# Weights, sums of squares and key products leave GpSimd for ScalarE and VectorE

## The chip, the cores and the metric

The kernel runs on one core of a Trainium2 chip. The metric is the device time of one launch in microseconds, as a median of several runs. TensorE is PE in the profile (its weight loads are PEld), VectorE is DVE, ScalarE is ACT, GpSimd is POOL and SyncE, which issues all of this kernel's DMAs, is SP.

## The reference

One inference step of a two-layer decoder trunk, in fp32, for a prompt of 1024 tokens and a group of 8 samples of 8 tokens; the model width is 1024. Every sub-layer is wrapped in two norms, and each layer ends in a feed-forward part (ffn) with a causal convolution of three taps:

```python
def rmsnorm(x, g):
    y = x32 * lax.rsqrt(jnp.mean(x32 * x32, axis=-1, keepdims=True) + EPS)
    return (y * g.astype(jnp.float32)).astype(x.dtype)

def conv_ffn(h, buf, w_up, dw_w, dw_b, w_down):          # D 1024, D_FF 2816
    up = h @ w_up
    c, buf_new = causal_dwconv(up, buf, dw_w, dw_b)
    g, val = jnp.split(c, 2, axis=-1)
    return (jax.nn.gelu(g) * val) @ w_down, buf_new

for layer in range(DEPTH):                               # in trunk
    h = rmsnorm(x, p['norm_pre_mix'][layer])
    y = even_mixer(...) if layer % 2 == 0 else odd_mixer(...)
    x = x + rmsnorm(y, p['norm_post_mix'][layer])
    h = rmsnorm(x, p['norm_pre_ffn'][layer])
    f, fb = conv_ffn(h, ...)
    x = x + rmsnorm(f, p['norm_post_ffn'][layer])
```

Layer 0's mixer is a gated linear attention (4 heads) beside a convolution of 31 taps over 512 channels; layer 1's is a dilated window attention in three groups (window 128, 512, 2048) beside a gated spatial product (gmlp). In layer 1 the samples' queries also meet the keys and values of three caches:

```python
s = jnp.einsum('bqhd,bqjhd->bqhj', qb, kv_sel[:, :, :, 0]) + bias_hj      # in dilated_attn
```

## The kernel before

The activations lie transposed, channels on the 128 partitions and tokens along the free axis. The tokens are worked in two halves: A is 512 tokens of the prompt; B is the other 512 and the 64 sample tokens, 576 columns, which every product takes in two pieces of 288.

**Products in fp32 from rounded parts.** Each product with a weight (`gemm`, L374) splits both operands into a rounded high part and the rest, and sums three products: high x high, low x high, high x low. The activations are split by `split` (L402: `hi` on ScalarE, `lo` on VectorE). The weights are split as they come, by `chunk` (L355) and `fill` (L363): the weight's DMA into `raw` (two buffers), the rounding into `whi` (three buffers), and the subtraction `wlo = raw - whi` (three buffers). A chunk is 128 x 1024 for an input or up projection, 128 x 512 or 128 x 384 for a down projection. Two counters out of 16 say which engine rounds and which subtracts: `hi_act` is the share of roundings on ScalarE (the rest go to GpSimd, `gts`, L206), `lo_pool` the share of subtractions on GpSimd (the rest go to VectorE). They change by stage in `run` (L1854): at the start 0 and 0; from the second part of the first input projection to the end of layer 0's ffn of A, 16 and 8; then 0 and 0; in layer 1's input projection of B, `hi_act` is 6; from the output projection of B in layer 1 to the end of layer 1's ffn of A, 16 and 16; then 0 and 0 to the end.

**Norms.** `sq_add` (L415) adds the squares of eight tiles for a norm: ScalarE squares, then a sum is added to a running tile `ss`. Where a half is not marked `urgent` there is one running tile, and GpSimd adds. Where it is marked, the norm is one that the next products wait for, and there are two running tiles, one added by GpSimd and one by VectorE. `rb` (L437) then multiplies each tile with a column of ones on TensorE, per block of 128 tokens, takes the reciprocal root (`rstd`, L229, on GpSimd) and spreads it. `last_down` (L644) does the sums for the last norm by itself, in two tiles, on GpSimd (L699).

**Keys of the cache.** `sample_scores` (L1676) multiplies cached keys `kc` with rows of queries on GpSimd (L1692) and reduces each product on VectorE (L1696). It runs beside layer 1's input projection of B, and its tiles come by DMA from the caches and from the queries in DRAM, up to `SA` tiles ahead.

**Order.** Work that is not a product of the main line (the convolution, linear attention, attention, norms) is a generator, woven between the products by `during` and `pump` (L236, L242) at a rate per product, and finished by `drain`. Each engine's order of instructions is then planned from estimated times, by priority; `chunk` puts its fills up to `ahead` = 400 places forward. On the chip every engine takes its list in that order.

Work that stays on GpSimd: small copies of the ffn's convolution edges (L600, L605, L606, L617, L618), the powers in `rstd`, scalings of the attention's scores (`gts` at L1466 and L1503), and memsets.

Of the kernel before, what the change touches and what calls it, by code (L numbers as in the profile page):

```python
# [9 lines left out]
F32 = mybir.dt.float32  # L10
# [3 lines left out]
ALU = mybir.AluOpType  # L14
# [124 lines left out]
class Kern:  # L139
    def __init__(self, ctx, tc, I, O):  # L140
        self.tc, self.nc, self.I, self.O = tc, tc.nc, I, O
        self.uid = 0
        pool = lambda name, **kw: ctx.enter_context(tc.tile_pool(name=name, **kw))
        self.cp = pool("cp", bufs=1)
        self.dp = pool("dp", bufs=1, space=DRAM)
        self.ar = [pool("arA", bufs=24), pool("arB", bufs=24)]
        self.wp = pool("wp", bufs=3)
        self.ap = pool("ap", bufs=10)
        self.fp = pool("fp", bufs=2)
        self.np_ = pool("np", bufs=1)  # L150
        self.mp = pool("mp", bufs=2)
        self.pg = pool("pg", bufs=4, space=PSUM)
        self.pm = pool("pm", bufs=4, space=PSUM)
        self.halves = [Half(0), Half(1)]
        self.rr = 0
        self.copy_act = False
        self.urgent = [0, 0]
        self.bg = None
        self.ahead = 0

        self.nw, self.hi_act, self.lo_pool = 0, 0, 0


    def nm(self, s):
# [197 lines left out]

    def fill(self, raw, whi, wlo, w, k0, nk, c0, m):  # L363
        self.wdma(raw[:, :nk, :m], w[k0 * P:(k0 + nk) * P, c0:c0 + m].rearrange("(k p) m -> p k m", p=P))
        self.nw += 1
        if self.nw * self.hi_act % 16 < self.hi_act:
            self.acopy(whi[:, :nk, :m], raw[:, :nk, :m])
        else:
            self.gts(whi[:, :nk, :m], raw[:, :nk, :m], 1.0, 0.0)
        eng = self.nc.gpsimd if self.nw * self.lo_pool % 16 < self.lo_pool else self.nc.vector  # L370
        eng.tensor_tensor(out=wlo[:, :nk, :m], in0=raw[:, :nk, :m], in1=whi[:, :nk, :m].bitcast(F32),  # L371
                          op=ALU.subtract)

    def gemm(self, h, hs, w, k0, c0, m):  # L374

# [38 lines left out]

    def sq_add(self, h, ss, src, k):  # L415

        if len(ss) <= k and len(ss) <= self.urgent[h.i]:
            ss.append(self.at(h, [P, h.n], name="ss") if self.urgent[h.i] else
                      self.np_.tile([P, h.n], F32, tag="ss", name=self.nm("ss"), bufs=2))
            self.act(ss[-1], src, AF.Square)  # L420
            return
        sq = (self.at(h, [P, h.n], name="sq") if self.urgent[h.i] else
              self.np_.tile([P, h.n], F32, tag="sq", name=self.nm("sq"), bufs=1))
        self.act(sq, src, AF.Square)
        t = ss[k % len(ss)]
        eng = self.nc.vector if k % len(ss) else self.nc.gpsimd
        eng.tensor_tensor(out=t, in0=t, in1=sq, op=ALU.add)  # L427

    def rms(self, h, src):

# [213 lines left out]
    def last_down(self, h, tmp, acts, l, part, y, xt):  # L644


        w = self.I["w_down"][l]
        nk = len(part)
        wts = []
        for m in range(KT):  # L650
            raw = self.wp.tile([P, 8, P], F32, tag="raw", name=self.nm("raw"), bufs=2)
            wt = [self.at(tmp if m < KT - 2 or not i else h, [P, nk, P], F32R, name="wt") for i in range(2)]
            self.fill(raw, wt[0], wt[1], w, part[0], nk, m * P, P)
            wts.append(wt)

        def rows(blocks, c1, sq):

            ps = self.psm()
            for b in blocks:
                c0, sz = h.blocks[b]  # L660
                for i, t in enumerate(sq):
                    self.mm(ps[:sz, b:b + 1], t[:, c0 - c1:c0 - c1 + sz], self.ones[:, :1], i == 0, i == len(sq) - 1)
            r = self.np_.tile([P, 8], F32, tag="r", name=self.nm("r"), bufs=2)
            full = [b for b in blocks if b < 4]
            self.rstd(r[:, full[0]:full[-1] + 1], ps[:, full[0]:full[-1] + 1], 1.0 / D)
            if 4 in blocks:
                self.rstd(r[:NS, 4:5], ps[:NS, 4:5], 1.0 / D)
            yield 1.0
            for b in blocks:
                c0, sz = h.blocks[b]  # L670
                for hf in range(2):
                    ps = self.psm()
                    for kk in range(4):
                        self.tr(ps[:sz, kk * P:(kk + 1) * P], y[hf * 4 + kk][:, c0:c0 + sz])
                    ob = self.at(h, [P, 512], name="ob")
                    self.stt(ob[:sz, :], ps[:sz, :], r[:sz, b:b + 1], xt[b][hf][:sz, :], ALU.mult, ALU.add)
                    if b < 4:
                        dst = self.O["y_prompt"][0, h.t0 + c0:h.t0 + c0 + sz, hf * 512:hf * 512 + 512]
                    else:
                        dst = self.O["y_sample"].rearrange("b s d -> (b s) d")[:, hf * 512:hf * 512 + 512]  # L680
                    self.dma(dst, ob[:sz, :])
                yield 1.0

        for blocks in ([2, 3, 4], [0, 1]):
            c1 = h.blocks[blocks[0]][0]
            cw = sum(h.blocks[b][1] for b in blocks)
            sqs = []
            for m in range(KT):
                ps = self.pg.tile([P, 512], F32, tag="g", name=self.nm("g"))
                for k in range(nk):  # L690
                    for j, (i, e) in enumerate(((0, 0), (0, 1), (1, 0))):
                        self.mm(ps[:, :cw], wts[m][i][:, k, :], acts[part[k]][e][:, c1:c1 + cw],
                                k == 0 and j == 0, k == nk - 1 and j == 2)
                yv = y[m][:, c1:c1 + cw]
                self.tt(yv, yv, ps[:, :cw], ALU.add)
                sq = self.at(h, [P, cw], name="sq")
                self.act(sq, yv, AF.Square)
                if m % 4:
                    self.nc.gpsimd.tensor_tensor(out=sqs[-1], in0=sqs[-1], in1=sq, op=ALU.add)  # L699
                else:  # L700
                    sqs.append(sq)
                self.acopy(yv, yv, self.v("norm_post_ffn", l * KT + m))
                self.pump(nk / 8 * cw / 512)
            self.during(rows(blocks, c1, sqs), len(blocks) + 1, 1.5)
        self.drain()
# [970 lines left out]
    def sample_scores(self, h, st):  # L1676


        nc = self.nc
# [3 lines left out]
        for stk in range(2):  # L1683
            sT = self.at(h, [P, 2, P], name="sT")
            st["sT"].append(sT)
            sv = sT.rearrange("p g (b h q) -> p g b h q", b=4, h=4)
            for bl in range(4):
                for z in range(4):
                    kc, qt = take(4 * stk + bl, 0, z)
                    for k, q in enumerate(qt):  # L1690
                        pr = self.wk(1 + (2 * z + k) % 4, [P, 512])
                        nc.gpsimd.tensor_tensor(out=pr, in0=kc.rearrange("p i c -> p (i c)"),  # L1692
                                                in1=q.rearrange("p i c -> p (i c)"), op=ALU.mult)
                        q0 = 2 * (z % 2) + 4 * k
                        dst = sv[:, z // 2, bl, :, q0:q0 + 2].rearrange("p h q -> p q h")
                        nc.vector.reduce_sum(out=dst, in_=pr.rearrange("p (i h d) -> p i h d", i=2, h=4), axis=AX.X)  # L1696
                        yield 1.0

            nc.vector.tensor_copy(sv[:, 1, :, :, 4:], sv[:, 1, :, :, :4])
# [154 lines left out]
    def run(self):  # L1854
# [27 lines left out]
        self.ahead = 400  # L1882
        self.drain()
        self.mix_consts()
        self.hi_act, self.lo_pool = 16, 8
        self.during(self.conv(A, st[0]), 90, 30)
        self.in_even(A, st[0]["hs"], st[0], ("glr", "q", "k", "v0", "v1", "r"))
        rest = self.merge((self.bg, 50), (self.gla(A, st[0]), 45))
# [17 lines left out]
        self.during(mix0(), 210, 61)  # L1906
        y, ss = self.ffn(A, hA, 0)
        self.drain()
        self.hi_act, self.lo_pool = 0, 0
        hA = []  # L1910
        self.urgent[0] = 1
        for _ in norms(A, y, ss, 1, "norm_post_ffn", 0, "norm_pre_mix", 1, hA):
# [41 lines left out]
        def odd_b():  # L1954
            self.drain()
            self.urgent = [0, 0]
            act = lambda shape: self.ap.tile(shape, F32, tag="act", name=self.nm("sg"))
            self.copy_act, self.hi_act = True, 6
            so[1] = self.in_odd(B, hB, lambda st: self.during(self.merge((self.gmlp(B, st, act), 11), (self.sample_scores(B, st), 48)), 59, QS))
            self.drain()  # L1960
            self.ffn_rows(0)
            self.copy_act, self.hi_act = False, 0
            self.during(mix1(B), QM, 45)

        def close_b():
            self.drain()
            self.hi_act, self.lo_pool = 16, 16
            y, ss = self.out_proj(B, so[1]["mo"], I["w_out_odd"][0])
            nxt["hB"] = []
            self.urgent[1] = 1  # L1970
# [2 lines left out]
        y, ss = self.ffn(A, nxt["hA"], 1, {0.5: odd_b, 4: close_b})  # L1973
        self.drain()
        self.urgent = [0, 0]
        self.hi_act, self.lo_pool = 0, 0
        rows = []

        def end_a():
# [34 lines left out]
```

## Time and profile before

| | us |
|---|---|
| median of 3 runs | 2743.83 |
| lowest, highest | 2738.05, 2746.66 |
| the profiled execution | 2735.78 |
| its span, first to last instruction | 2733.9 |
| mean granted clock of TensorE | 0.97 |

A line of the profile names a source line, an engine, an operation and the tiles it writes and reads (`out<-in`), with the count behind an x. "Idle before" and "waits" say how long an engine stood before an instruction and what released it. PEclk, or the clock in a window, is the share of full speed that TensorE was granted. A window is a stretch of the span in us.

### The profile page before, as it was taken

Reading aid. Unit: us, or ns where it says so; the run is one execution under the profiler, and the core shown is the slowest. Engines: PE = TensorE matmul, PEld = TensorE weight load, DVE = VectorE, ACT = ScalarE, POOL = GpSimd, SP = SyncE. Lnnn points to the kernel's source line nnn. Section 1 sums busy time; section 2 is a strip of 40 time slices with the busy share of each in tenths; the row PEclk is TensorE's granted clock in tenths of the full one; section 3 lists DMA queues with packets and bytes.
Section 4 is the critical chain, followed back from the end, with each engine's and each line's share of the span. In section 5 each row is a group of like instructions: output and inputs, shape, how many; then the busy total and the mean of one; then the engine's idle time right before and its main releaser. Section 6 shows DMA issues by size and latency. Waiting matters only on the chain.

```text
span 2733.9 us, 43963 instructions
## 1 busy us (share of the span) xinstructions
PE 2601.8 (95%) x16517; PEld 2327.2 (85%) x16517; DVE 1753.5 (64%) x3065; ACT 961.9 (35%) x2022; POOL 1023.1 (37%) x1139
## 2 busy tenths in 40 slices
PE   7989999999999999999999999889999898999998
PEld 6779787787888779999999979878878678999998
DVE  4897359999677653655557784547665358555555
ACT  4343445443453222333323242113333343322223
POOL 2311333342235443243437533553113266333333
PEclk9999989999999999999999999999999799999999
DMA  7433354454544454332324336884454152422232
GB/s 218 127 99 92 90 188 151 138 159 159 179 142 126 152 179 117 117 97 81 89 70 137 122 112 191 234 237 133 131 162 137 34 172 84 140 78 75 81 91 82
DMA packets 505004, 355.83 MB, mean 130 GB/s; under 512 B 29547, under 2 KB 461282, under 8 KB 504015
## 3 DMA queue, kind: packets, MB, share of 16 engines
q1 hardware_dynamic: 504791, 353.01, 42.7%
q8 instruction: 131, 2.15, 0.3%
q14 instruction: 82, 0.67, 0.1%
HBM read 306.43 MB, written 75.97 MB: 140 GB/s over the span
## 4 chain that ended last, share of the span: by engine, by line
PE 73%; DVE 10%; DMA 7%; POOL 4%; issue 3%; ACT 2%; SPq 1%; DVEq 0%; POOLq 0%; ACTq 0%
PE g L227 65%; PE m L227 7%; DVE cv L200 3%; PE m L224 2%; DMA kc<-qr 2%; DVE wlo L371 1%; SPq L188 1%; POOL whi L206 1%; DVE y L200 1%; DVE c L200 1%; POOL ss L427 1%; POOL w L1692 1%; DVE lo L197 1%; DVE y L197 1%; POOL wlo L371 1%
## 5 line engine op out<-in xcount | busy, mean ns | idle before, releaser
L227 PE MATMUL g<-hi,whi 128*128 128x288 f32 (+2 forms) x4440 | 1276.7, 336 | 25.7 <-DVE y L197 9.3
L227 PE MATMUL g<-lo,whi 128*128 128x288 f32 (+2 forms) x4440 | 1263.5, 333 | 5.4 <-DVE lo L197 5.3
L227 PE MATMUL g<-hi,wlo 128*128 128x288 f32 (+1 forms) x4416 | 1254.4, 333 | 9.8 <-POOL wlo L371 6.6
L227 PEld LDWEIGHTS g<-hi,whi 128*128 128x128 f32 (+1 forms) x4440 | 776.5, 191 | 100.0 <-issue 25.9
L227 PEld LDWEIGHTS g<-lo,whi 128*128 128x128 f32 (+1 forms) x4440 | 775.3, 191 | 69.2 <-DVE lo L197 7.5
L227 PEld LDWEIGHTS g<-hi,wlo 128*128 128x128 f32 x4416 | 771.5, 191 | 72.5 <-POOL wlo L371 7.0
L371 DVE TENSOR_TENSOR wlo<-raw,whi 128x1024 fp32r<-128x1024 f32 (+2 forms) x382 | 408.1, 1069 | 443.0 <-POOL whi L206 346.1
L206 POOL TENSOR_SCALAR whi<-raw 128x1024 fp32r<-128x1024 f32 (+2 forms) x307 | 313.7, 1022 | 708.8 <-PE g L227 589.2
L371 POOL TENSOR_TENSOR wlo<-raw,whi 128x1024 fp32r<-128x1024 f32 (+2 forms) x94 | 205.0, 2182 | 417.0 <-ACT whi L209 357.1
L200 DVE SCALAR_TENSOR_TENSOR c<-u,dw,c 128x512 f32<-128x512 f32 (+3 forms) x528 | 318.7, 641 | 47.1 <-ACT c L212 45.7
L209 ACT ACTIVATE whi<-raw 128x1024 fp32r<-128x1024 f32 (+3 forms) x171 | 145.1, 849 | 362.8 <-PE g L227 189.4
L209 ACT ACTIVATE u<-g 128x224 f32<-128x224 f32 (+2 forms) x352 | 128.7, 397 | 299.9 <-PE g L227 286.4
L200 DVE SCALAR_TENSOR_TENSOR cv<-u,cvw,cv 128x512 f32<-128x512 f32 (+21 forms) x240 | 193.3, 815 | 1.8
L197 DVE TENSOR_TENSOR y<-y,g 128x288 f32<-128x288 f32 (+3 forms) x240 | 120.3, 526 | 107.2 <-PE g L227 106.9
L212 ACT ACTIVATE c<-g,dw 128x288 f32<-128x288 f32 (+1 forms) x264 | 172.9, 657 | 2.6 <-DVE lo L197 1.5
L427 POOL TENSOR_TENSOR ss<-ss,sq 128x512 f32<-128x512 f32 (+1 forms) x75 | 120.8, 1611 | 42.7 <-ACT sq L212 41.4
L209 ACT ACTIVATE hi<-c 128x512 fp32r<-128x512 f32 (+1 forms) x88 | 57.9, 658 | 209.1 <-DVE c L197 208.7
L212 ACT ACTIVATE c<-c 128x512 f32<-128x512 f32 (+1 forms) x88 | 57.9, 658 | 142.2 <-DVE c L200 138.3
L600 POOL COPY last<-u 128x2 f32<-128x2 f32 x88 | 49.9, 568 | 120.8 <-ACT u L209 118.0
L200 DVE SCALAR_TENSOR_TENSOR y<-y,vec,rb 128x512 f32<-128x512 f32 (+1 forms) x104 | 88.3, 915 | 7.1 <-ACT rb L209 7.1
L212 ACT ACTIVATE sq<-y 128x512 f32<-128x512 f32 (+3 forms) x103 | 63.1, 622 | 82.9 <-POOL ss L427 43.9
L1692 POOL TENSOR_TENSOR w<-kc,kc 128x512 f32<-128x512 f32 x48 | 65.2, 1372 | 70.7 <-DMA kc<-qr 58.6
(288 smaller groups left out, 2208.7 us busy)
## 6 DMA issues: line engine op xcount, KB each, us to landing
raw<-in_w_up SPq DMA_DIRECT2D x176, 512.0 KB
raw<-in_w_down SPq DMA_DIRECT2D x128, 256.0 KB
raw<-in_w_in_odd SPq DMA_DIRECT2D x44, 512.0 KB
raw<-in_w_in_even SPq DMA_DIRECT2D x40, 512.0 KB
out_s_kv<-in_cache_c_w SPq DMA_DIRECT2D x32, 512.0 KB
raw<-in_w_down SPq DMA_DIRECT2D x64, 192.0 KB
xl<-x SPq DMA_DIRECT2D x40, 256.0 KB
kc<-in_cache_c_w SPq DMA_DIRECT2D x80, 128.0 KB
```

Source lines behind the costliest of these rows:

```text
L188: self.nc.sync.dma_start(out, in_)
L197: self.nc.vector.tensor_tensor(out=out, in0=a, in1=b, op=op)
L200: self.nc.vector.scalar_tensor_tensor(out=out, in0=a, scalar=s, in1=b, op0=op0, op1=op1)
L206: self.nc.gpsimd.tensor_scalar(out=out, in0=a, scalar1=s1, scalar2=s2, op0=op0, op1=op1)
L209: self.nc.scalar.activation(out, in_, AF.Copy, scale=scale)
L212: self.nc.scalar.activation(out, in_, func, **kw)
L224: self.nc.tensor.transpose(out, in_, self.ident[:k, :k])
L227: self.nc.tensor.matmul(out, l, r, start=start, stop=stop)
L371: eng.tensor_tensor(out=wlo[:, :nk, :m], in0=raw[:, :nk, :m], in1=whi[:, :nk, :m].bitcast(F32), op=ALU.subtract)
L427: eng.tensor_tensor(out=t, in0=t, in1=sq, op=ALU.add)
L600: self.nc.gpsimd.tensor_copy(self.last2[l][:, jt, :], u[:, 512:514])
L1692: nc.gpsimd.tensor_tensor(out=pr, in0=kc.rearrange("p i c -> p (i c)"), in1=q.rearrange("p i c -> p (i c)"), op=ALU.mult)
```

## The change

All roundings of weights go to ScalarE and all their subtractions to VectorE, whatever the stage, and the two counters go. A norm has one running tile in all cases, and VectorE adds to it; so it does in `last_down`. The keys' products go to VectorE.

```diff
     def fill(self, raw, whi, wlo, w, k0, nk, c0, m):
         self.wdma(raw[:, :nk, :m], w[...].rearrange("(k p) m -> p k m", p=P))
-        self.nw += 1
-        if self.nw * self.hi_act % 16 < self.hi_act:
-            self.acopy(whi[:, :nk, :m], raw[:, :nk, :m])
-        else:
-            self.gts(whi[:, :nk, :m], raw[:, :nk, :m], 1.0, 0.0)
-        eng = self.nc.gpsimd if self.nw * self.lo_pool % 16 < self.lo_pool else self.nc.vector
-        eng.tensor_tensor(out=wlo[:, :nk, :m], in0=raw[:, :nk, :m], in1=whi[:, :nk, :m].bitcast(F32),
-                          op=ALU.subtract)
+        self.acopy(whi[:, :nk, :m], raw[:, :nk, :m])
+        self.tt(wlo[:, :nk, :m], raw[:, :nk, :m], whi[:, :nk, :m].bitcast(F32), ALU.subtract)
...
     def sq_add(self, h, ss, src, k):
-        if len(ss) <= k and len(ss) <= self.urgent[h.i]:
+        if not ss:
...
-        t = ss[k % len(ss)]
-        eng = self.nc.vector if k % len(ss) else self.nc.gpsimd
-        eng.tensor_tensor(out=t, in0=t, in1=sq, op=ALU.add)
+        self.tt(ss[0], ss[0], sq, ALU.add)
...
                 if m % 4:                                   # last_down
-                    self.nc.gpsimd.tensor_tensor(out=sqs[-1], in0=sqs[-1], in1=sq, op=ALU.add)
+                    self.tt(sqs[-1], sqs[-1], sq, ALU.add)
...
                         pr = self.wk(1 + (2 * z + k) % 4, [P, 512])      # sample_scores
-                        nc.gpsimd.tensor_tensor(out=pr, in0=kc..., in1=q..., op=ALU.mult)
+                        self.tt(pr, kc..., q..., ALU.mult)
```

The lines of `run` that set `hi_act` and `lo_pool` go as well.

More of the change, by code (lines that the diff above doesn't have):

```diff
@@ L159, in __init__ @@
         self.ahead = 0
-        self.nw, self.hi_act, self.lo_pool = 0, 0, 0
     def nm(self, s):
@@ L1691, in sample_scores @@
                         pr = self.wk(1 + (2 * z + k) % 4, [P, 512])
-                        nc.gpsimd.tensor_tensor(out=pr, in0=kc.rearrange("p i c -> p (i c)"),
-                                                in1=q.rearrange("p i c -> p (i c)"), op=ALU.mult)
+                        self.tt(pr, kc.rearrange("p i c -> p (i c)"), q.rearrange("p i c -> p (i c)"), ALU.mult)
                         q0 = 2 * (z % 2) + 4 * k
@@ L1884, in run @@
         self.mix_consts()
-        self.hi_act, self.lo_pool = 16, 8
         self.during(self.conv(A, st[0]), 90, 30)
@@ L1908, in run @@
         self.drain()
-        self.hi_act, self.lo_pool = 0, 0
         hA = []
@@ L1957, in odd_b @@
             act = lambda shape: self.ap.tile(shape, F32, tag="act", name=self.nm("sg"))
-            self.copy_act, self.hi_act = True, 6
+            self.copy_act = True
             so[1] = self.in_odd(B, hB, lambda st: self.during(self.merge((self.gmlp(B, st, act), 11), (self.sample_scores(B, st), 48)), 59, QS))
@@ L1961, in odd_b @@
             self.ffn_rows(0)
-            self.copy_act, self.hi_act = False, 0
+            self.copy_act = False
             self.during(mix1(B), QM, 45)
@@ L1966, in close_b @@
             self.drain()
-            self.hi_act, self.lo_pool = 16, 16
             y, ss = self.out_proj(B, so[1]["mo"], I["w_out_odd"][0])
@@ L1975, in run @@
         self.urgent = [0, 0]
-        self.hi_act, self.lo_pool = 0, 0
         rows = []
```

## The prediction

> **What bounds the kernel now.** I read the page's engine totals first, then its slices, then the waits of TensorE, then stretches of time.
>
> ```profile
> span 2733.9 us, 43963 instructions
> PE 2601.8 (95%) x16517; PEld 2327.2 (85%) x16517; DVE 1753.5 (64%) x3065; ACT 961.9 (35%) x2022; POOL 1023.1 (37%) x1139
> ...
> PEclk9999989999999999999999999999999799999999
> ```
>
> TensorE is the bound: 95% of the span, the next engine 64%. Only its holes (132 us) and its slow stretches (the slices with a 7, 8 or 9 for the clock) can be won; work of the other engines costs something only where it makes a hole. Both kinds of stretch, and the places that matter below, by windows (width; busy PE, PEld, DVE, ACT, POOL; granted clock; DMA):
>
> ```profile
> 375.00:389.00 14.00, 11.07 (x52) 10.83 (x51) 3.34 (x5) 1.66 (x3) 6.98 (x4) 0.63 0.81 278
> 536.00:550.00 14.00, 7.38 (x21) 5.55 (x20) 12.00 (x22) 4.04 (x8) 10.99 (x5) 0.63 0.35 114
> 883.00:902.00 19.00, 13.65 (x76) 13.18 (x75) 11.28 (x9) 2.08 (x4) 12.96 (x9) 0.73 0.32 102
> 2234.00:2254.00 20.00, 16.48 (x62) 13.25 (x61) 16.02 (x24) 9.79 (x17) 12.66 (x14) 0.74 0.65 223
> 410.00:684.00 274.00, 260.19 (x1293) 209.98 (x1292) 262.77 (x475) 117.62 (x193) 94.86 (x57) 0.96 0.47 152
> 684.00:820.00 136.00, 136.00 (x689) 112.18 (x687) 90.58 (x163) 64.66 (x128) 40.69 (x46) 1.00 0.51 160
> 1709.00:1845.00 136.00, 116.79 (x778) 108.04 (x777) 70.62 (x119) 25.70 (x66) 69.69 (x61) 0.95 0.85 236
> 2330.00:2660.00 330.00, 329.10 (x2478) 328.79 (x2477) 175.45 (x298) 93.08 (x230) 116.29 (x205) 1.00 0.31 91
> ```
>
> The last row has 330 us with no hole at all: nothing can be won there. The first four are the places where TensorE waits for GpSimd. Who it waits for, by its own waits (total us, times, longest):
>
> ```profile
> PE g L227 <- DVE y L197: 10.6, 5, 4.1
> PE m L227 <- POOL ss L427: 9.8, 3, 3.5
> PE g L227 <- ACT hi L209: 6.7, 4, 3.0
> PE g L227 <- POOL wlo L371: 6.6, 1, 6.6
> PE g L227 <- ACT c L212: 6.1, 2, 5.2
> ```
>
> Each of those waits is paid twice: behind it the clock is granted at less than full. In the four windows the share missing is 0.37x14, 0.37x14, 0.27x19 and 0.26x20, that is 5.2 us of full speed in each.
>
> **Why those waits exist.** The costliest forms of what moves, with mean ns (line, engine, shape, count | busy us, mean ns | idle before), then the subtraction's durations (shortest, median, longest, all and in 410 to 684) and single instructions (start, us):
>
> ```profile
> L371 DVE TENSOR_TENSOR wlo<-raw,whi 128x1024 fp32r<-128x1024 f32 x230 | 307.3, 1336 | 333.1 <-POOL whi L206 245.6 <-ACT whi L209 71.8 <-DMA raw<-in_w_in_odd 9.2
> L206 POOL TENSOR_SCALAR whi<-raw 128x1024 fp32r<-128x1024 f32 x179 | 225.3, 1259 | 422.9 <-PE g L227 338.5 <-DMA raw<-in_w_in_odd 24.6 <-DMA raw<-in_w_in_even 19.5
> L371 POOL TENSOR_TENSOR wlo<-raw,whi 128x1024 fp32r<-128x1024 f32 x46 | 145.2, 3157 | 262.1 <-ACT whi L209 252.5 <-PE m L227 8.6 <-PE g L227 0.9
> L209 ACT ACTIVATE whi<-raw 128x1024 fp32r<-128x1024 f32 x97 | 102.7, 1059 | 242.2 <-PE g L227 119.5 <-DMA raw<-in_w_up 60.0 <-DMA raw<-in_w_in_even 21.9
> L371 POOL TENSOR_TENSOR wlo<-raw,whi x94: 995/1852/13077, 68.9 to 2272.3; 128x1024 fp32r<-128x1024 f32 x46, 128x512 fp32r<-128x512 f32 x24, 128x384 fp32r<-128x384 f32 x24
> L371 POOL TENSOR_TENSOR wlo<-raw,whi x27: 1264/2397/13077, 418.4 to 679.0; 128x1024 fp32r<-128x1024 f32 x15, 128x512 fp32r<-128x512 f32 x12
> 530.56 13.08 POOL L371 TENSOR_TENSOR wlo<-raw,whi 128x1024 fp32r<-128x1024 f32 x1 [4.26 <-ACT whi L209]
> 526.74 1.21 DVE L371 TENSOR_TENSOR wlo<-raw,whi 128x1024 fp32r<-128x1024 f32 x1
> L200 DVE SCALAR_TENSOR_TENSOR cv<-us,cvw,cv 128x64 f32<-128x64 f32 x120 | 57.5, 479 | 0.0
> 539.71 0.27 DVE L200 SCALAR_TENSOR_TENSOR cv<-us,cvw,cv 128x64 f32<-128x64 f32 x1
> 541.36 2.35 DVE L200 SCALAR_TENSOR_TENSOR cv<-us,cvw,cv 128x64 f32<-128x64 f32 x1
> ```
>
> The same subtraction takes 1.21 us on VectorE and up to 13.08 on GpSimd, and the same VectorE step of the convolution takes 0.27 us or 2.35: the two engines hold each other up, in whole instructions. The 13.08 us one is what TensorE stood for at 537.
>
> **The change, part by part.**
>
> *Rounding (whi) to ScalarE.* 307 instructions leave GpSimd. A whole weight takes 1.059 us on ScalarE and 1.259 on GpSimd, collisions among them. ScalarE gains at most 307x1.059 = 325 us and rises from 35% to 47%. Where ScalarE already rounds every weight (684 to 820, and 410 to 684), TensorE is busy for all 136 us of the first; the second has a cause of its own, below. So the rounding is covered by ScalarE's free half; were the cover gone, as where ScalarE is behind, each weight would come 1.06 us later. It has a price in the queue: ScalarE now also stands for a free weight buffer and for the weight's DMA, with PSUM evictions, activations and softmax behind it, and TensorE behind those. The nearest rows are TensorE's waits for ScalarE, 6.7 + 6.1 us: they could double, +13, or go, -13, as wlo comes sooner. They are few today in stretches of both kinds, so I take +3.
>
> *Subtraction (wlo) to VectorE.* 94 instructions, at most 94x1.336 = 126 us, nearer 46x1.21 + 48x0.68 = 88 undisturbed. By the code half of a weight's subtractions up to the end of layer 0's first FFN are GpSimd's, and all of them around the last output projection. In 410 to 684, with 27 of them, VectorE is 96% busy, so cover is thin: what hides the added work there is the time that its own collisions give back, at 479 against 270 ns over 120 steps, 25 us, and 1336 against 1210 over 230, 29 us. I put added and freed VectorE time as equal, 0, with +15 us as the upper end (the rival below). What goes is the stall at 537: 6.6 + 5.2 = 11.8 us. Next late there is the same chunk's wlo on VectorE behind at most two 0.7 us steps, well ahead. Gain -11.8, bounds -11.8 to 0.
>
> *Sums of squares to VectorE, one per norm.* The rows that carry it: GpSimd's adds, a clean VectorE add of that shape, and one urgent norm in the two timelines:
>
> ```profile
> L427 POOL TENSOR_TENSOR ss<-ss,sq 128x512 f32<-128x512 f32 x41 | 62.9, 1535 | 27.2 <-ACT sq L212 26.1 <-DMA raw<-in_w_out_odd 0.9
> L197 DVE TENSOR_TENSOR y<-y,xl 128x512 f32<-128x512 f32 x32 | 20.0, 680 | 0.0
> 365.49 4.89 DVE L197 TENSOR_TENSOR y<-y,xl 128x512 f32<-128x512 f32 x8
> 365.93 7.33 POOL L371 TENSOR_TENSOR wlo<-raw,whi 128x1024 fp32r<-128x1024 f32 x1 [11.14 <-ACT whi L209]
> 373.22 5.60 POOL L427 TENSOR_TENSOR ss<-ss,sq 128x512 f32<-128x512 f32 x3
> L227 PE MATMUL m<-ones,ss x152: 163/251/373, 350.2 to 2296.0; 128*128 128x1 f32 x136, 128*64 128x1 f32 x16
> L212 ACT ACTIVATE ss<-y x17: 612/635/702, 311.0 to 2267.8; 128x512 f32<-128x512 f32 x9, 128x576 f32<-128x576 f32 x8
> ```
>
> 75 adds at about 0.7 us put 53 us on VectorE, 12 shorter ones at the end some 6. Outside the urgent norms VectorE has room and ScalarE stops waiting for GpSimd's add: 0. In the urgent norm shown, the y additions run to 370.4 and GpSimd ends the sums at 378.8. After: 4.89 + 7 adds x 0.68 + two wlo of 1.21 = 12.1 us behind 365.5, so 377.6: only 1.3 us earlier, because seven adds now stand in one line where two engines shared them. The stretch loses 3.1 us of wait, so about 40% goes. The three waits and the three stretches behind them are 9.8 + 3x5.2 = 25.4 us; 40% is -10, bounds 0 (VectorE no faster) to -25. One sum per norm also means fewer products with the ones: 17 first tiles for 13 sums, so four norms were double, two of four and two of five blocks, two records each: 36 of 152 go, at 0.15 to 0.25 us some 5 to 9, about half of them in places where TensorE waits anyway: -3.
>
> *Keys' products to VectorE.* 48 of them:
>
> ```profile
> L1692 POOL TENSOR_TENSOR w<-kc,kc 128x512 f32<-128x512 f32 x48 | 65.2, 1372 | 70.7 <-DMA kc<-qr 58.6 <-DMA zq<-qkv 3.8 <-DMA kn<-zk 2.6
> POOL whi L206 <- PE g L227: 589.2, 207, 11.4
> POOL whi L206 <- DMA raw<-in_w_in_odd: 24.6, 4, 12.0
> POOL whi L206 <- DMA raw<-in_w_in_even: 19.5, 6, 13.0
> POOL whi L206 <- DMA raw<-in_w_down: 15.5, 10, 3.0
> POOL whi L206 <- DMA raw<-in_w_up: 14.3, 7, 5.8
> ```
>
> At 0.68 they put 33 us on VectorE between 1640 and 1845, busy 70.6 of 136 in most of it; the multiply waits for the DMA of its rows (58.6 us), whose share there is 0.85, and the transfers stay. A key buffer is free about 0.6 us sooner, so the DMA queue behind it moves up, into the same full DMA. A product waiting for its rows now holds up VectorE's wlo and evictions. Taken 0, since DMA stays the bound; bounds -3 to +8 (the 58.6 us of waits, times the 19 of 136 us in which TensorE is idle there).
>
> *What follows elsewhere.* TensorE's waits for "DVE y" (10.6 us) and the clock behind them shrink where VectorE's steps were held: -6, bounds 0 to -16 (10.6 and one stretch of 5.2). GpSimd keeps the halo copies, reciprocal roots and scalings, with an emptier queue: 0.
>
> **The sum.** -11.8 - 10 - 3 - 6 + 3 = -28 on the profiled execution's 2733.9 (its own time 2735.8): 2708. That execution is 8 us under the median of the runs, 2743.8; I add half of that, so 2712, or 1.1% under the median.
>
> **Rivals.**
> 1. *ScalarE's queue stands for weights* (slower). Today GpSimd alone stands for late weight transfers: 24.6 + 19.5 + 15.5 + 14.3 = 74 us. ScalarE would stand there with PSUM's evictions behind it, above all in the odd input projection, where the DMA share is 0.85. For it: 12.0 and 13.0 us waits exist. Against: the weights whose transfer is late hold TensorE too, and in 684 to 820 ScalarE rounds all with no hole. If all of it reaches TensorE: 2712 + 74 = 2786; half: 2749. From 40 us on the gain is gone and slower by 0.3% (8 us) begins. Chance 0.17.
> 2. *VectorE becomes the bound of the convolution stretches* (no change). If the collisions stay, because the small copies hold the port as well, 410 to 684 needs 262.8 + 15x1.21 + 12x0.68 = 289 of 274, +15; the norms and the y steps gain nothing: 2712 + 15 + 10 + 6 = 2743. For it: the 96%. Against: the 2.35 and 13.08 us rows stand beside large GpSimd work. Chance 0.17. The Trainium skill, "SBUF — State Buffer", section Who interferes with whom, has the collision as an exclusive lock between a GpSimd instruction that reads SBUF and a VectorE one with two SBUF inputs, whoever starts first, whatever its size. By that rule the copies that stay do collide; the two rows of 0.27 and 2.35 us agree with a lock, and no row here shows one held by a copy alone.
> 3. *All waits for GpSimd and for slowed VectorE steps go*: -11.8 - 25 - 16 - 3 = -56, so 2684. Chance 0.14. The Trainium skill, "GPSIMD Engine Reference", section Engine selection, speaks against a part of the change: one-input work runs on GpSimd at about line rate, only two-input work at about half of VectorE's. By it the rounding's move brings nothing and the -6 for freed steps falls away, an estimate of 2718; the 1.26 us of GpSimd's roundings, with their collisions, against ScalarE's 1.06 fit that in size.
>
> **How the numbers follow.** Forecast 0.52, rivals 0.17, 0.17, 0.14. A measurement of this kernel tells no change from one of 0.3%, about 8 us. Faster: the forecast and rival 3, 0.66; slower: rival 1, 0.17; the same: rival 2, 0.17. The range goes from 2682 (rival 3) to 2750 (rival 2, and rival 1 at half); within the forecast alone it is 2695 to 2728.
>
> **What would show it.** Right: GpSimd's busy time near 300 us and no wlo, whi or ss on it; VectorE near 1750 to 1900 us, its cv step at 64 columns back near 0.27; ScalarE near 1230; the windows at 537 and 890 at full clock; no wait of TensorE for POOL wlo or ss. Wrong: new TensorE waits for ACT u, c or hi behind an ACT wait for "DMA raw"; VectorE above 68 of 68 in the convolution with TensorE waiting for DVE wlo or lo; holes in the last ffn, which has none today.

## The result and the profile after

The changed kernel takes 2670.83 us (median of 4 runs, 2665.69 to 2676.52) against 2745.24 for the kernel before in the same series of runs: a ratio of 0.9737, interval 0.9714 to 0.976, or 2.6% faster. That is below the predicted range (2682 to 2750); the sign was right, the gain more than twice the forecast's. In the profiled executions the span went from 2733.9 to 2674.6 us, 59 us less.

The page of the changed kernel, totals and slices:

```profile
span 2674.6 us, 43712 instructions
PE 2588.3 (97%) x16481; PEld 2314.9 (87%) x16481; DVE 1751.2 (65%) x3299; ACT 1212.8 (45%) x2341; POOL 308.6 (12%) x594
...
DVE  4898479999677546455558774656655478455556
...
PEclk9999999999999999999999999999989899999999
```

GpSimd fell from 1023 to 309 us, ScalarE rose by 251, both about as forecast. VectorE has 234 instructions more and is as busy as before (1751.2 against 1753.5 us). TensorE's waits of this execution (total us, times, longest), in their order:

```profile
PE m L222 <- DMA rows<-in_ln_b_b: 12.0, 1, 12.0
PE m L225 <- DVE kt L195: 10.5, 4, 5.7
PE g L225 <- DVE lo L195: 7.5, 6, 3.2
PE g L225 <- DVE y L195: 6.1, 4, 3.2
PE g L225 <- ACT hi L207: 5.2, 5, 2.0
PE m L222 <- POOL S L204: 5.1, 1, 5.1
```

The waits for a wlo of GpSimd (6.6 us) and for its sums (9.8 us) are gone; those for VectorE's sums and wlo come to 3.1 and 0.8 us. Now the forms that moved, and the convolution's 64-column step, in the groups kept apart by shape (count | busy us, mean ns):

```profile
L195 DVE TENSOR_TENSOR wlo<-raw,whi 128x1024 fp32r<-128x1024 f32 x276 | 337.6, 1223 | 323.3 <-ACT whi L207 317.8 <-PE m L225 2.5 <-issue 0.2
L207 ACT ACTIVATE whi<-raw 128x1024 fp32r<-128x1024 f32 x276 | 292.4, 1060 | 622.4 <-PE g L225 508.4 <-DMA raw<-in_w_up 76.2 <-DMA raw<-in_w_in_odd 12.7
L195 DVE TENSOR_TENSOR ss<-ss,sq 128x512 f32<-128x512 f32 x49 | 33.7, 688 | 2.5 <-ACT sq L210 2.1
L198 DVE SCALAR_TENSOR_TENSOR cv<-us,cvw,cv 128x64 f32<-128x64 f32 x120 | 32.0, 274 | 0.1
```

VectorE's steps shown here run at their clean durations: wlo 1223 ns (1336 before), the convolution step 274 (479 before). Where that counted is seen in the convolution stretch of layer 0's first ffn, from the first down projection's weights to the same later weight, in each kernel's own time: before, then after (columns as in the prediction's windows).

```profile
449.00:690.00 241.00, 227.19 (x1135) 183.12 (x1134) 230.33 (x421) 95.19 (x159) 81.71 (x49) 0.96 0.47 151
```

```profile
424.00:649.00 225.00, 224.62 (x1190) 182.69 (x1187) 215.93 (x444) 98.21 (x168) 40.08 (x26) 1.00 0.53 165
```

VectorE is 96% busy in both. The stretch became 16 us shorter and VectorE's busy time there 14 us, although it now does 48 subtractions in place of 25. Before, VectorE had hardly any time to spare there, and TensorE was idle or slowed for part of it. After, TensorE has no hole left and the full clock, so a still faster VectorE would gain nothing more. By the start of each stage's weights, layer 0's input projection up to the first weight of the output projection became 13 us shorter (246 to 233), the first ffn of A with everything beside it 30 us (477 to 447), and all the rest together 16.

### The profile page after: what moved, and what is told of

It reads as the page before. It is cut to its first block, busy times and chain, and to the rows that moved or that the text cites. A ratio compares the mean times of both kernels' runs of the same rounds, so it can differ in the third digit from the quotient of the medians.

```text
span 2674.6 us, 43712 instructions
## 1 busy us (share of the span) xinstructions
PE 2588.3 (97%) x16481; PEld 2314.9 (87%) x16481; DVE 1751.2 (65%) x3299; ACT 1212.8 (45%) x2341; POOL 308.6 (12%) x594
## 4 chain that ended last, share of the span: by engine, by line
PE 84%; DMA 5%; DVE 5%; ACT 3%; issue 1%; SPq 1%; POOL 0%; DVEq 0%; POOLq 0%; ACTq 0%
PE g L225 75%; PE m L225 7%; PE m L222 2%; DMA kc<-qr 2%; DMA raw<-in_w_down 1%; DVE y L198 1%; DVE wlo L195 1%; SPq L186 1%; DVE y L195 1%; ACT whi L207 1%; DMA xb<-in_x_prompt 0%; DMA kc<-in_cache_c_w 0%; DVE w L195 0%; DVE c L198 0%; ACT L210 0%
## 5 line engine op out<-in xcount | busy, mean ns | idle before, releaser
L207 ACT ACTIVATE whi<-raw 128x1024 fp32r<-128x1024 f32 (+3 forms) x478 | 413.0, 865 | 928.5 <-PE g L225 743.5
L195 DVE TENSOR_TENSOR wlo<-raw,whi 128x1024 fp32r<-128x1024 f32 (+2 forms) x476 | 468.5, 985 | 441.0 <-ACT whi L207 434.7
L198 DVE SCALAR_TENSOR_TENSOR c<-u,dw,c 128x512 f32<-128x512 f32 (+3 forms) x528 | 293.6, 592 | 54.5 <-ACT c L210 51.2
L198 DVE SCALAR_TENSOR_TENSOR cv<-u,cvw,cv 128x512 f32<-128x512 f32 (+16 forms) x240 | 172.7, 734 | 1.2
L590 POOL COPY last<-u 128x2 f32<-128x2 f32 x88 | 83.0, 945 | 706.9 <-ACT u L207 706.9
L207 ACT ACTIVATE u<-g 128x224 f32<-128x224 f32 (+2 forms) x352 | 127.2, 392 | 23.9 <-PE g L225 16.3
L607 POOL COPY lastp<-u 128x2 f32<-128x2 f32 x88 | 30.2, 343 | 457.5 <-ACT u L207 457.5
L195 DVE TENSOR_TENSOR lo<-c,hi 128x512 fp32r<-128x512 f32 (+1 forms) x88 | 63.8, 725 | 23.2 <-ACT hi L207 23.0
L231 POOL TENSOR_TENSOR r<-r,mhalf 128x4 f32<-128x4 f32 (+2 forms) x25 | 28.1, 1135 | 420.3 <-DVE r L201 420.3
L198 DVE SCALAR_TENSOR_TENSOR y<-y,vec,rb 128x512 f32<-128x512 f32 (+1 forms) x104 | 73.6, 775 | 0.6 <-ACT rb L207 0.5
L195 DVE TENSOR_TENSOR ss<-ss,sq 128x512 f32<-128x512 f32 (+1 forms) x91 | 64.9, 718 | 8.9 <-ACT sq L210 8.3
```

Source lines behind the costliest of these rows:

```text
L195: self.nc.vector.tensor_tensor(out=out, in0=a, in1=b, op=op)
L198: self.nc.vector.scalar_tensor_tensor(out=out, in0=a, scalar=s, in1=b, op0=op0, op1=op1)
L207: self.nc.scalar.activation(out, in_, AF.Copy, scale=scale)
L231: self.nc.gpsimd.tensor_tensor(out=out, in0=out, in1=self.mhalf[:p, :n], op=ALU.pow)
L590: self.nc.gpsimd.tensor_copy(self.last2[l][:, jt, :], u[:, 512:514])
L607: self.nc.gpsimd.tensor_copy(self.lastp[:, :, jt], u[:, 512:514])
```

## The experiments

**One part at a time.** Four kernels, each the kernel before with one part of the change. Each series of runs has its own runs of the kernel before to compare with. The engines' orders are planned anew for each kernel, so every part brings a new order with it.

Subtractions alone:

```diff
-        eng = self.nc.gpsimd if self.nw * self.lo_pool % 16 < self.lo_pool else self.nc.vector
-        eng.tensor_tensor(out=wlo..., in0=raw..., in1=whi..., op=ALU.subtract)
+        self.tt(wlo..., raw..., whi..., ALU.subtract)
```

> The kernel before with every subtraction of a weight on VectorE, nothing else changed. Theory C (collisions): most of the change's 59 us of span is VectorE no longer being held up by GpSimd's two-input instructions in layer 0, where the 94 subtractions were: about -40 us against the kernel before, nearly all of it before the second layer's input projection. Theory D (GpSimd's own lateness): only the waits that TensorE had for a late subtraction go: about -12 us. Theory N (the norms): next to nothing, -5 us.

Measured: 2690.25 us against 2736.8, ratio 0.9822 (0.9795 to 0.9849): 47 us, theory C's size and four times D's. 39 of the 45 us by which its span is shorter lie in layer 0's input projection and first ffn, 17 of them in the convolution stretch.

Roundings alone:

```diff
-        if self.nw * self.hi_act % 16 < self.hi_act:
-            self.acopy(whi..., raw...)
-        else:
-            self.gts(whi..., raw..., 1.0, 0.0)
+        self.acopy(whi..., raw...)
```

> The kernel before with every rounding of a weight on ScalarE, nothing else changed. Theory C: GpSimd's roundings read SBUF as well and held VectorE up by less, -5 to -15 us, in the stretches behind layer 0's first ffn. Theory D: 0, since TensorE hardly waited for a rounding. Theory Q (ScalarE's queue stands for weights): +5 to +15 us, in the ffn that runs beside layer 1's attention of half B.

Measured: 2725.34 us, 0.9967 (0.9955 to 0.998): 11 us, as C said. Its totals:

```profile
PE 2608.9 (96%) x16517; PEld 2329.0 (86%) x16517; DVE 1702.4 (63%) x3065; ACT 1211.3 (44%) x2341; POOL 684.4 (25%) x824
```

VectorE has exactly the 3065 instructions of before and is busy 51 us less: that is what GpSimd's one-input roundings had cost it, as far as the new order has no share in it. Of those 51 only 11 reach the end. Most of them lie behind layer 0's first ffn, where VectorE was busy for 37 to 77% of each stage; that this is the reason fits, and isn't shown. The ffn of A in layer 1 up to the output projection's end, where theory Q looked, is 9 us longer (399 to 408).

Norms alone:

```diff
-        if len(ss) <= k and len(ss) <= self.urgent[h.i]:
+        if not ss:
...
-        eng = self.nc.vector if k % len(ss) else self.nc.gpsimd
-        eng.tensor_tensor(out=t, in0=t, in1=sq, op=ALU.add)
+        self.tt(ss[0], ss[0], sq, ALU.add)          # and the same in last_down
```

> The kernel before with one running sum per norm, added by VectorE, nothing else changed. Theory C: -5 to -10 us (the adds of GpSimd collided with the norms' own steps on VectorE). Theory D: -10 to -25 us, the waits for the sums and the clock behind them. Theory N: -25 us or more.

Measured: 2709.81 us, 0.9904 (0.9883 to 0.9925): 27 us. That is more than C said, just above D's range and within N's, so this run alone does not tell them apart.

Keys alone, the one line of `sample_scores`:

> The kernel before with the products of the cached keys on VectorE, nothing else changed. Theories C and D: 0, within 5 us, since the transfers of the rows set the pace there. Theory V (VectorE late in that stretch): +5 to +10 us.

Measured: 2740.47 us, 1.0015 (0.9997 to 1.0032): no change that can be told. By medians the four parts are 47 + 11 + 27 - 4 = 81 us; together they gave 66 to 74, so they overlap a little.

**Collisions or late results?** The subtractions' move does two things besides the new order: VectorE is no longer held up, and wlo no longer comes late from GpSimd. Two kernels put GpSimd's work back without its results. VectorE computes every wlo, and GpSimd does idle work on tiles of the same size at the same places, 95 with a small 128 x 128 weight that the prediction's row of 94 leaves out. All but 192 of TensorE's 16517 instructions stand at the same place in its order as without the idle work:

```diff
+        if self.nw * self.lo_pool % 16 < self.lo_pool:
+            x = whi[:, :nk, :m].bitcast(F32)
+            self.nc.gpsimd.tensor_tensor(out=self.scr[:, :nk, :m], in0=x, in1=x, op=ALU.subtract)
```

> The kernel with all subtractions on VectorE (and nothing else of the change), and beside each of the 94 that were GpSimd's an idle GpSimd instruction of the same size with two SBUF inputs: the rounded weight minus itself into a scratch tile in bf16 that nothing reads. VectorE still computes every wlo, and the engines' orders stay as without it. Theory C (GpSimd's two-input work holds VectorE up): 25 to 47 us of the 47 us that the subtractions' move won come back, and VectorE's steps in layer 0 are long again (its 64-column convolution step near 0.45 us). Theory D (TensorE waited for GpSimd's late results): nothing comes back, within 5 us.

Measured: 2723.58 us against 2736.95, 0.9955 (0.9938 to 0.9971): 33 of the 47 us come back though nothing reads what GpSimd does. In the second the idle work has one input:

```diff
+            for _ in range(2):
+                self.gts(self.scr[:, :nk, :m], whi[:, :nk, :m].bitcast(F32), 1.0, 0.0)
```

> The same, with two idle GpSimd instructions of one SBUF input each (a multiplication of the rounded weight by 1) in place of one with two. Theory C with a port held by any GpSimd instruction that reads: 15 to 45 us come back. Theory C2 (only two-input work of GpSimd collides): nothing, within 5 us. Theory D: nothing.

Measured: 2722.23 us, 0.9943 (0.9925 to 0.996): 32 us come back. Totals of the subtractions alone, then with two-input and with one-input idle work:

```profile
PE 2589.2 (96%) x16517; PEld 2317.5 (86%) x16517; DVE 1755.0 (65%) x3160; ACT 965.5 (36%) x2022; POOL 845.8 (31%) x1044
```

```profile
PE 2596.7 (95%) x16517; PEld 2320.0 (85%) x16517; DVE 1819.4 (67%) x3160; ACT 966.1 (35%) x2022; POOL 1024.7 (38%) x1139
```

```profile
PE 2595.3 (95%) x16517; PEld 2319.7 (85%) x16517; DVE 1814.0 (67%) x3160; ACT 965.4 (35%) x2022; POOL 1062.0 (39%) x1234
```

The same 3160 VectorE instructions take 64 and 59 us longer. And the convolution stretch, without and with two-input idle work, again from the same weight to the same weight:

```profile
431.00:655.00 224.00, 223.78 (x1181) 182.09 (x1180) 215.72 (x443) 97.99 (x168) 41.40 (x26) 1.00 0.51 166
```

```profile
443.00:685.00 242.00, 229.47 (x1179) 183.17 (x1178) 237.18 (x445) 99.28 (x170) 90.22 (x50) 0.99 0.48 154
```

It grows by 18 us as VectorE's busy time there grows by 21. The rows of the idle run show who holds whom (groups by shape):

```profile
L374 POOL TENSOR_TENSOR scr<-whi 128x1024 bf16<-128x1024 f32 x46 | 144.3, 3137 | 286.3 <-ACT whi L209 285.4 <-ACT k L209 0.7
L200 DVE SCALAR_TENSOR_TENSOR cv<-us,cvw,cv 128x64 f32<-128x64 f32 x120 | 43.2, 366 | 0.1
```

A GpSimd instruction whose result nobody uses takes 3137 ns on average (1892 at the shortest), and VectorE's 64-column step takes 366 ns in place of 275, less than the 450 expected. So GpSimd's reading alone accounts for about 33 of the 47 us, in theory C's range. Not all of it need be VectorE held up: the idle work also stands ahead of GpSimd's own sums, and TensorE's waits for those rose from 2.1 to 5.2 us. The other 14 us can be late results, the new order, or the idle work being lighter than the subtraction (1892 ns against 2342 at the shortest for a whole weight); no run isolates them.

Nor is VectorE's busy time all that sets the convolution stretch. In the kernel with two sums per norm on VectorE (below), where GpSimd still subtracts, the stretch and TensorE's longest wait in it are:

```profile
447.00:694.00 247.00, 228.79 (x1141) 183.19 (x1140) 224.79 (x417) 94.63 (x158) 87.18 (x49) 0.96 0.46 148
PE g L227 <- POOL wlo L371: 14.8, 4, 7.5
```

VectorE is busy for less there than before (225 against 230 us), and yet the stretch is 6 us longer: late results of GpSimd cost time too.

**The norms: one sum, or another engine?** Two sums are kept and VectorE adds both:

```diff
-        eng = self.nc.vector if k % len(ss) else self.nc.gpsimd
-        eng.tensor_tensor(out=t, in0=t, in1=sq, op=ALU.add)
+        self.tt(t, t, sq, ALU.add)
```

> The kernel before with the norms' running sums all added by VectorE, but still two sums in the urgent norms (so the same products with the ones). The run with one sum per norm on VectorE was 27 us faster than before. Theory C: what counts is that GpSimd no longer adds, so 20 to 27 us here as well. Theory P (the fewer products with the ones and the shorter end of the norm): 5 to 15 us here, the rest is the single sum.

Measured: 2716.31 us against 2737.45, 0.9918 (0.9895 to 0.994), 21 us; the intervals of one sum and two overlap. The engine makes most of it. Then one sum on VectorE, with an idle GpSimd addition at each of the 75 places:

```diff
+        if not self.urgent[h.i] or k > 1 and k % 2 == 0:
+            self.nc.gpsimd.tensor_tensor(out=self.scr[:, :h.n], in0=src, in1=src, op=ALU.add)
```

> The kernel before with one sum per norm on VectorE, and beside each of the 75 additions that were GpSimd's an idle GpSimd addition of the same size, of the tile whose square is summed to itself, into scratch that nothing reads. Theory C: 10 to 27 of the 27 us come back. Theory D (TensorE and ScalarE waited for GpSimd's late sums): within 5 us of the run with one sum, 0.990 of before.

Measured: 2749.19 us, 1.0042 (1.003 to 1.0055): all of the 27 us come back, and 12 more, for VectorE now has every addition and the collisions as well. The first urgent norm, VectorE's timeline (start, us) with one sum and then with the idle additions beside it:

```profile
364.35 4.91 DVE L197 TENSOR_TENSOR y<-y,xl 128x512 f32<-128x512 f32 x8
369.17 3.51 DVE L197 TENSOR_TENSOR ss<-ss,sq 128x512 f32<-128x512 f32 x2
372.60 1.21 DVE L371 TENSOR_TENSOR wlo<-raw,whi 128x1024 fp32r<-128x1024 f32 x1
373.74 3.66 DVE L197 TENSOR_TENSOR ss<-ss,sq 128x512 f32<-128x512 f32 x5
```

```profile
364.23 4.90 DVE L197 TENSOR_TENSOR y<-y,xl 128x512 f32<-128x512 f32 x8
369.05 3.50 DVE L197 TENSOR_TENSOR ss<-ss,sq 128x512 f32<-128x512 f32 x2
372.47 2.06 DVE L372 TENSOR_TENSOR wlo<-raw,whi 128x1024 fp32r<-128x1024 f32 x1
374.45 7.28 DVE L197 TENSOR_TENSOR ss<-ss,sq 128x512 f32<-128x512 f32 x5
```

The last five additions take 7.28 us in place of 3.66, and the sum is ready at 381.7 in place of 377.4. TensorE waits 2.3 us for just that end, and not at all with one sum alone. So what GpSimd reads here costs 39 us between the two runs, though nobody needs it, and mostly by collisions: TensorE's waits for GpSimd's own wlo and whi grew by only 3 us (9.8 to 12.8). How the 27 us divide in the kernel before, where GpSimd's sums were needed and VectorE had fewer additions, this doesn't say.

**Can the changed kernel be bettered?** The keys' products back on GpSimd; then, beside it, the roundings on GpSimd while layer 1's attention of B runs:

> The changed kernel with the products of the cached keys back on GpSimd. Theory V (VectorE late in layer 1's input projection of B when it has the products): 3 to 8 us faster than the changed kernel, a ratio to before near 0.971. Theory C: 3 us slower than it, since the products collide on GpSimd again.

> As the run with the keys back, and with GpSimd rounding the weights again while layer 1's attention of half B runs beside the ffn. Theory Q (ScalarE's queue stands for weights, with the attention's exponentials behind): that stretch loses its extra 9 us, a ratio to before near 0.968. Theory C: 0 to 5 us slower than with the keys back.

Measured: 2671.76 us, 0.9767 (0.9737 to 0.9796), and 2671.92 us, 0.9771 (0.9734 to 0.9808). The changed kernel again:

> The changed kernel again, on the chip of these runs, to stand beside them and beside the one with the keys back: 2671 us, a ratio near 0.974.

Measured: 2671.49 us against 2737.45, 0.9763 (0.9742 to 0.9783). All three are the same within their intervals: there is no sign of theory V, though its lower end of 3 us is too small to exclude, and theory Q's 9 us in that stretch aren't won back. At last the attention's scalings on ScalarE:

```diff
-                    self.gts(s[:, 256:], s[:, 256:], wt[:, 1, e, x:x + 1], 0.0)
+                    self.acopy(s[:, 256:], s[:, 256:], wt[:, 1, e, x:x + 1])     # and the group before
```

> The changed kernel with the 64 scalings of the attention's scores on ScalarE as well, so that GpSimd keeps only small copies, reciprocal roots and memsets. TensorE waits 5.1 us for one of them, with the clock down behind it. Theory D: 3 to 10 us faster than the changed kernel. Theory C: 0 to 3 us, since these one-input steps of 0.55 us collide little. Theory Q: slower by up to 5 us, ScalarE having the exponentials in that stretch.

Measured: 2677.93 us, 0.9781 (0.9762 to 0.98): 6 us over the changed kernel by medians, with overlapping intervals. TensorE's wait for a GpSimd scaling became one for ScalarE's, 4.6 us, and it waits for a rounding as well:

```profile
PE g L225 <- ACT whi L207: 4.7, 2, 4.3
...
PE m L222 <- ACT S L207: 4.6, 1, 4.6
```

No version beat the changed kernel.

## Why the prediction was wrong

*Where the bound is.* The prediction took TensorE as the bound everywhere and counted little besides TensorE's named waits and the clock behind them. In the convolution stretch VectorE had as good as no free time: 230 us busy in 241 before, 237 in 242 with idle work on GpSimd, and 216 in 225 after, when TensorE too is without a hole. The prediction saw the 96% and used it only as a risk. The Trainium skill, "Perfetto Trace Analysis", Optimization Strategy, says that the most contended engine can change over a kernel's time; the windows agree with it, and the prediction read the shares once for the span.

*Added and freed VectorE time, set equal: the step that failed.* Over the whole kernel it was right to 2 us (1753.5, then 1755.0 with the subtractions moved), and its two rows of freed time, 25 and 29 us, came out at 25 and 26. But time is won in the stretch that has none to spare, and the sum was not made there. With the subtractions alone moved, the 48 there take 45.5 us in place of 23.9 for 25, which adds 22; yet VectorE's busy time fell by 15, so 36 us left. Some 28 of these are shorter steps: the 64-column step gave about 19, the 512-column step (815 ns before, 740 after), which the prediction left out, 7. The other 8 are 12 convolution steps that the new order puts outside the stretch. So the prediction set at 0 what was a net gain in the place where it counts, and the stretch became 17 us shorter. The whole term, -11.8 us, measured 47; 13 us of that lie in layer 0's input projection and 8 in the first ffn ahead of the stretch, where no run says which steps carried it.

*Norms.* Forecast 10 + 3 = 13 us, measured alone 27. The step that failed is the serial sum for the urgent norm, which was to be ready 12.1 us after the y additions begin, against 13.3 before. It was ready after 13.0 (364.35 to 377.4), so hardly sooner; VectorE's first two additions still took 3.51 us beside a subtraction on GpSimd. TensorE's wait of 2.9 us went all the same, because in the new order TensorE comes to its products with the ones only at 379.4. So the forecast's way to the gain is not the one that was seen. About 16 of the 25 us of span lie in the three stages with the waits for a sum, and the idle additions show what collisions cost there; the share of the new order stays open. The 36 products with the ones went as forecast (16517 to 16481).

*Roundings.* Forecast +3 for the queue, and -6 for VectorE's freed steps from all parts together; measured alone -11. ScalarE's free half did cover them: in the last ffn TensorE has 330.0 of 330 us with ScalarE rounding everything. *Keys:* forecast 0, measured 4 us slower by medians, which the interval does not tell from none.

*Rivals.* The first (ScalarE stands for weights) did not happen: TensorE's waits for ScalarE stayed small (5.2 us for hi, the largest in total), and giving the roundings back in the attention stretch changed nothing. The second expected the small copies to keep VectorE held: with all of them still there its steps run clean (274 ns). The third, all waits gone, -56 us, was nearest, but for a reason too narrow: the time lay not only in waits with a name, but also in a stretch in which VectorE had no free time.

The idle one-input reads of GpSimd held VectorE as the two-input ones did (59 and 64 us). The lock that the Trainium skill, "SBUF — State Buffer", Who interferes with whom, describes between the two engines is in agreement with these runs. Its use for the forecast would have been to ask what VectorE's clean durations add up to in the stretch where it is the bound.

What stays open: the stretch of layer 1's attention of B is 4 to 10 us longer in the kernels with the roundings or the keys moved, and no run explains it. Nor does any run hold the engines' orders as they were before and move only the work, so what the planning anew gave or took is not known.

## What to carry to other kernels

Look for the bound by stretch, and there add up the busy time of the engine that has none to spare, at its clean durations. Work of GpSimd that reads SBUF was not free here even where nobody waited for it. Compare VectorE's clean and mean durations per form: the difference times the count is a fair estimate of what leaves with GpSimd's work (25 us forecast and measured for the 64-column step). Idle work in place of the moved work helps to tell a collision from a late result, as long as it delays little else on its own engine.

## What the runs showed of the hardware

GpSimd work that reads SBUF cost VectorE 64 us of busy time for 95 two-input instructions and 59 us for 190 one-input ones on the same tiles. GpSimd is held up too: the idle subtraction of a whole weight took 3.1 us on average and 1.9 at the shortest, and one subtraction in the kernel before took 13.08 us beside a full VectorE queue, against 2.34 at the shortest on GpSimd and 1.22 on VectorE.
